# First quad of a two-layer GEGLU kernel: six of its eight weight pieces by casting transfers on the Pool queue, instead of fp32 transfers and casts on chip

## Chip, cores, metric

One core of one Trainium2 chip. The metric is device microseconds (us) of one execution.

## The reference

```python
gate = x @ w_gate                       # x: 8192 tokens x 1024, w_gate, w_up: 1024 x 4096
up = x @ w_up
gate = 0.5 * gate * (1 + np.tanh(np.sqrt(2 / np.pi) * (gate + 0.044715 * gate ** 3)))
h = gate * up
return (h @ w_down).astype(np.float32)  # w_down: 4096 x 1024; all float32
```

## The kernel before

Tokens go through in eight passes of 1024. In the first passes the products are built by a seven-product scheme: it multiplies sums and differences of blocks of x and of the weights. Weight columns are handled in quads of 512 (gate and up each), a quad is two pairs of 256 columns. Only the first quad of the first pass is special, because nothing is on the chip yet: pair 0 is computed by plain products as its pieces arrive, pair 1 already by the scheme, for which VectorE must form sums of x (`sum_x`) and of weights (`sum_w`).

All pieces of that quad are 512 KB of fp32. They come on one hardware queue (issued by SyncE): eight of x, and eight of the weights (gate or up, upper or lower half of K, first or second 256 columns). The weights are staged as fp32 and cast to fp16 by ScalarE or VectorE. Every later quad comes by a transfer that casts on the way, issued by GpSimd (`load_raw`); such a transfer goes through the Pool queue. A one-element GpSimd copy out of a staged piece holds the Pool queue until that piece has landed: a gate.

```python
    def load_first(w, kh, cols):                      # fp32 piece, hardware queue
        nc.sync.dma_start(
            out=staging0(w, kh)[:, :, cols], in_=w_v[w][:, kh * KH : (kh + 1) * KH, cols]
        )

    def cast_first(w, kh, cols, copy=nc.scalar.copy, ks=slice(0, KH)):
        o = raw(0, 0)[:, w, kh * KH : (kh + 1) * KH, cols]
        copy(o[:, ks], staging0(w, kh)[:, ks, cols])
    ...
        # first_pair(): c0, c1 = first, second 256 columns
        ...
        x0_transpose(0, 0, 1, 5, act)
        x0_cast(0, 1, 1)
        x0_transpose(0, 1, 1, 7, dve)
        halves(1)                                     # gate, lower K, c0: cast on ScalarE
        product(1, 0, 1, 0)
        cast_first(1, 1, c0, dve)                     # up, lower K, c0: cast on VectorE
        product(0, 1, 0, 0)                           # first product that needs the lower K
        ...
        for w in range(2):
            cast_first(w, 0, c1)
        nc.gpsimd.tensor_copy(mark, staging0(1, 0)[:, 0, 256:257])   # gate
        load_raw(0, 1)                                # next quad, casting
        ...
        cast_first(0, 1, c1)
        cast_first(1, 1, c1, dve)
        ...
        sum_x(1)
        sum_w(0, 1, 0)
        sum_w(0, 1, 1)
        sum_x(2)
        ...
    # order on the hardware queue
    for kh in range(2):
        for gp in range(2):
            x0_load(0, gp, kh)
        for w in range(2):
            load_first(w, kh, slice(0, 256))
        for gp in range(2):
            x0_load(1, gp, kh)
    for kh in range(2):
        for w in range(2):
            load_first(w, kh, slice(256, 512))
```

## Time and profile before

| | before |
|---|---|
| first three runs | 2253.45, 2254.71, 2254.88 us |
| span of the profiled run | 2252.9 us |
| TensorE busy | 2245.2 us |
| pair 1 starts | 26.80 us |
| last fp32 piece landed (VectorE's wait ends) | 27.61 us |
| the mark M (below) | 38.37 us |
| last piece of the down product of pass 0 starts | 279.21 us |

A line of the timeline holds the start in us, the length in us, engine, source line, operation, output and inputs, and in brackets the idle time before it and what ended it. In these lines `x_b` is x in fp16, `x_sums` its sums and differences, `ring` the buffers of the fp16 weights and of their sums, and `ps` the banks that hold products; `h_a` and `x_sums` also serve as staging for the fp32 pieces. A busy TensorE is not TensorE at its peak, so I compare starts, not busy times. Two starts serve as marks through the whole document. M is the start of the sixteen matmuls with which pair 1 ends and pair 2 begins (eight each); from there to about 279 us the order of work is the same in all kernels. This is M in the timeline of TensorE of the kernel before:

```profile
38.37 3.62 PE L635 MATMUL ps<-x_b,ring 128*128 128x512 f16 x16
```

The second mark is the start at 279 us, the only later point at which TensorE waits in this trace. From it to the last VectorE instruction are 1970.4 us. So M and the start at 279 us tell nearly all that a change in the first quad can do; what is left in the time beside them is the last store and the run itself.

### The profile page before, as it was taken

To read this page: it belongs to the slowest core of one execution; us is meant where nothing else is said; L and a number is where in the kernel's file an instruction comes from. 1 tells how busy PE (TensorE), PEld (TensorE's weight loads), DVE (VectorE), ACT (ScalarE), POOL (GpSimd) and SP (SyncE) were. 2 spreads that over 40 slices of the span, in tenths; PEclk is the share of its full clock that TensorE was granted. 3 is DMA by queue.
4 is the path that set the end of the run, shared out by engine and by line. 5 is a ranking of instruction groups with operands and counts; after the bars stand their busy time and mean duration, and the time that the engine had idled before them with its cause. 6 is when DMAs were issued, how large, how long until landed. Compare 5 with 4: busy or idle time off the path is not lost.

```text
span 2252.9 us, 42769 instructions
## 1 busy us (share of the span) xinstructions
PE 2245.2 (100%) x16616; PEld 1624.1 (72%) x16616; DVE 1560.6 (69%) x2189; ACT 956.4 (42%) x1863; POOL 680.6 (30%) x825
## 2 busy tenths in 40 slices
PE   9999999999999999999999999999999999999999
PEld 4444444444444445888888888888888888888888
DVE  6666458883588755777776677666776667866674
ACT  4443135651355622666125550356404653055520
POOL 1332013330133200555014550255402543044520
PEclk9999999999999999999999999999999999999999
DMA  9898969989999999999998999989999889988876
GB/s 243 164 209 216 288 180 242 262 267 289 247 227 249 279 311 348 328 350 363 302 337 278 316 300 321 321 270 324 307 327 316 286 308 318 318 315 275 283 289 232
DMA packets 309133, 642.46 MB, mean 285 GB/s; under 512 B 79104, under 2 KB 185344, under 8 KB 288384
## 3 DMA queue, kind: packets, MB, share of 16 engines
q1 hardware_dynamic: 254144, 566.57, 73.5%
q0 software_dynamic: 54784, 73.14, 19.3%
q8 instruction: 130, 2.13, 0.4%
q14 instruction: 75, 0.61, 0.1%
HBM read 574.36 MB, written 138.41 MB: 316 GB/s over the span
## 4 chain that ended last, share of the span: by engine, by line
PE 87%; DMA 2%; SPq 1%; DVE 0%; issue 0%; DVEq 0%
PE ps L857 40%; PE ps L1108 20%; PE ps L635 17%; PE ps L1000 10%; DMA wd_quads<-x_sums 1%; SPq L255 0%; DMA ring<-wd_ops 0%; PE ps L1130 0%; DVE x_sums L278 0%; DVE h_a L932 0%; DVE tmp L1140 0%; SPq L496 0%; DVEq L278 0%; SPq L544 0%
## 5 line engine op out<-in xcount | busy, mean ns | idle before, releaser
L857 PEld LDWEIGHTS <-ring 128*128 128x128 f16 x8320 | 814.1, 98 | 94.4
L834 POOL TENSOR_TENSOR h_a<-tmp 128x256 f16<-128x256 f32 x640 | 469.2, 752 | 839.1 <-ACT tmp L822 831.9
L857 PE MATMUL ps<-x_sums,ring 128*128 128x256 f16 x5760 | 655.8, 273 | 0.0
L819 DVE TENSOR_TENSOR tmp<-tmp,ps 128x512 f32<-128x512 f32 x640 | 414.3, 683 | 148.2 <-PE ps L857 100.7
L635 PEld LDWEIGHTS <-ring 128*128 128x128 f16 x2632 | 257.4, 98 | 311.9 <-issue 1.1
L804 ACT COPY tmp<-ps 128x512 f32<-128x512 f32 x520 | 304.5, 586 | 236.7 <-PE ps L857 164.4
L635 PE MATMUL ps<-x_sums,ring 128*128 128x512 f16 x1504 | 340.1, 379 | 0.6 <-DVE x_sums L267 0.4
L822 ACT ACTIVATE tmp<-tmp 128x256 f32<-128x256 f32 x640 | 264.3, 418 | 172.6 <-DVE tmp L817 79.2
L857 PE MATMUL ps<-x_b,ring 128*128 128x256 f16 x2560 | 305.6, 273 | 0.0
L817 DVE TENSOR_TENSOR tmp<-ps,tmp 128x512 f32<-128x512 f32 x240 | 165.4, 689 | 145.2 <-ACT tmp L804 99.9
L635 PE MATMUL ps<-x_b,ring 128*128 128x512 f16 x1128 | 259.3, 379 | 0.1
L661 POOL TENSOR_TENSOR h_a<-tmp 128x512 f16<-128x512 f32 x94 | 145.5, 1548 | 372.9 <-ACT tmp L659 265.6
L1108 PEld LDWEIGHTS <-h_a 128*128 128x128 f16 x2208 | 216.0, 98 | 25.0
L1000 PE MATMUL ps<-ring,h_a 128*128 128x512 f16 x1024 | 222.3, 379 | 0.7 <-DMA ring<-wd_ops 0.7
L1108 PE MATMUL ps<-ring,h_a 128*128 128x256 f16 x1888 | 212.6, 273 | 0.0
L1000 PEld LDWEIGHTS <-h_a 128*128 128x128 f16 x1152 | 112.7, 98 | 136.8 <-DMA ring<-wd_ops 1.2
L654 DVE TENSOR_TENSOR tmp<-ps,tmp 128x512 f32<-128x512 f32 x188 | 127.2, 684 | 113.7 <-ACT tmp L646 112.2
L1238 ACT ACTIVATE tmp<-ps 128x512 f32<-128x512 f32 x60 | 35.3, 598 | 362.5 <-PE ps L1108 274.5
L1171 DVE SCALAR_TENSOR_TENSOR tmp<-ps,tmp 128x512 f32<-128x512 f32 x119 | 80.4, 690 | 95.0 <-PE ps L1108 64.1
L360 DVE TENSOR_TENSOR ring<-ring 128x1024 f16<-128x1024 f16 x188 | 137.6, 745 | 10.5 <-DMA ring<-in_w_up_dram 6.2
L646 ACT COPY tmp<-ps 128x512 f32<-128x512 f32 x188 | 109.8, 586 | 78.5 <-PE ps L635 78.5
L1108 PE MATMUL ps<-ring,x_sums 128*128 128x256 f16 x1120 | 126.3, 273 | 0.0
(105 smaller groups left out, 1538.0 us busy)
## 6 DMA issues: line engine op xcount, KB each, us to landing
ring<-w_ops SPq DMA_DIRECT2D x480, 512.0 KB, 4.8
ring<-wd_quads SPq DMA_DIRECT2D x110, 1024.0 KB, 7.1
ring<-wd_ops SPq DMA_DIRECT2D x35, 1024.0 KB, 7.9
w_ops<-h_s SPq DMA_DIRECT2D x128, 256.0 KB, 6.7
out_dram<-tmp SPq DMA_DIRECT2D x127, 256.0 KB, 6.3
ring<-in_w_gate_dram POOLq DMA_DIRECT2D x23, 1024.0 KB, 10.4
ring<-in_w_up_dram POOLq DMA_DIRECT2D x23, 1024.0 KB, 18.0
wd_quads<-x_sums SPq DMA_DIRECT2D x131, 128.0 KB, 6.6
```

The source lines that it names most:

```text
L360: nc.vector.tensor_tensor(o, a, b, op)
L635: nc.tensor.matmul(ps(b, w), lhs[:, k], rhs[:, k, :], start=(first and k == 0), stop=(k == KH - 1), skip_group_check=True,)
L654: nc.vector.tensor_tensor(o, ps("b", w), o, ADD)
L661: nc.gpsimd.tensor_tensor(hq[TO[n]][:, i, :], tmp[:, t[n, 1]], tmp[:, t[n, 0]], MUL)
L804: nc.scalar.copy(tmp[:, t[o[1]]], ps_all[:, bank[o[2]]])
L817: nc.vector.tensor_tensor(d, b, a, SUB)
L819: nc.vector.tensor_tensor(d, a, b, ADD if o[4] == "add" else SUB)
L822: nc.scalar.activation(d, d, GELU, scale=GSC)
L834: nc.gpsimd.tensor_tensor(h, tmp[:, t[o[1]], MQ : 2 * MQ], g, MUL)
L857: nc.tensor.matmul(ps_all[:, bank[c], w * MQ : (w + 1) * MQ], lhs[:, w, k], rhs[:, k], start=(first and w == 0 and k == 0), stop=(k == KH ...
L1000: nc.tensor.matmul(ps_all[:, bank[b, g]], lhs[:, j, g * P : (g + 1) * P], dc[:, n, :], start=(first and j == 0), stop=(j == NP - 1), skip_ ...
L1108: nc.tensor.matmul(ps_all[:, bank[c], m * MQ : (m + 1) * MQ], lhs[:, j, m * P : (m + 1) * P], rhs[:, j, :], start=(first and j == 0 and m ...
```

## The change

The intent: free ScalarE and VectorE of most casts of the first quad, and let the Pool queue start early instead of after the first quad. Upper K of the first columns stays fp32 on the hardware queue; the other six weight pieces become casting transfers behind two gates, and the next quad's load follows them without a gate.

```diff
+    def load_cast(w, kh, cols):
+        nc.gpsimd.dma_start(
+            out=raw(0, 0)[:, w, kh * KH : (kh + 1) * KH, cols],
+            in_=w_v[w][:, kh * KH : (kh + 1) * KH, cols],
+        )
...
+        nc.gpsimd.tensor_copy(mark, staging0(1, 0)[:, 0, 0:1])
+        for w in range(2):
+            load_cast(w, 1, c0)
+        nc.gpsimd.tensor_copy(mark, x0_f32[1][:, 0, KH * P : KH * P + 1])
+        for kh in range(2):
+            for w in range(2):
+                load_cast(w, kh, c1)
+        load_raw(0, 1)
         warm(7)
...
-        halves(1)
         product(1, 0, 1, 0)
-        cast_first(1, 1, c0, dve)
...
-        for w in range(2):
-            cast_first(w, 0, c1)
-
-        nc.gpsimd.tensor_copy(mark, staging0(1, 0)[:, 0, 256:257])
-        load_raw(0, 1)
...
-        cast_first(0, 1, c1)
-        cast_first(1, 1, c1, dve)
...
-        for w in range(2):
-            load_first(w, kh, slice(0, 256))
+        for w in range(2 if kh == 0 else 0):
+            load_first(w, 0, slice(0, 256))
...
-    for kh in range(2):
-        for w in range(2):
-            load_first(w, kh, slice(256, 512))
```

## The prediction

> **What bounds the kernel now.** I read the page first, then the chain that ended last, then the first 45 us by engine, because everything that the change touches lies there.
>
> ```profile
> PE 2245.2 (100%) x16616; PEld 1624.1 (72%) x16616; DVE 1560.6 (69%) x2189; ACT 956.4 (42%) x1863; POOL 680.6 (30%) x825
> PEclk9999999999999999999999999999999999999999
> ```
>
> TensorE is busy for 2245.2 of 2252.9 us at the full granted clock. All its idle time is 7.7 us, so a change that leaves the matmuls alone can win little. The chain of waits says that it is TensorE all the way from 279 us on, back to back:
>
> ```profile
> 229.17 1.14 DVE h_a L932
> ...
> 270.81 8.35 DMA ring<-wd_ops
> 279.16 0.05 issue
> 279.21 27.80 PE ps L1000 x128
> 307.01 193.39 PE ps L635 x896
> ```
>
> Two readings. First, 193.39 us for 896 matmuls is 0.216 us each; a pair of gate/up columns (56 matmuls) costs 12.1 us when nothing stalls it. Second, one wait (0.7 us, at 279.2 us) hangs on a transfer whose own chain goes back to VectorE work at 229 us. VectorE is busy without a gap there and is itself fed by TensorE's progress, so I take it that a shift made in the first 40 us moves this chain along, rather than being swallowed by it.
>
> The waits of TensorE over the whole run:
>
> ```profile
> PE ps L1284 <- DVE h_s L1287: 1.6, 1, 1.6
> PE ps L314 <- DVE h_a L304: 0.7, 1, 0.7
> PE ps L1000 <- DMA ring<-wd_ops: 0.7, 1, 0.7
> PE ps L1263 <- ACT x_b L317: 0.7, 1, 0.7
> PE ps L635 <- DVE x_sums L267: 0.4, 1, 0.4
> PE ps L635 <- DVE ring L360: 0.2, 1, 0.2
> ```
>
> The last three are in the first quad (the first 512 columns, pairs 0 and 1), and the last two are what the change can reach. "Busy" hides part of them, so I take starts from the timeline of TensorE and VectorE:
>
> ```profile
> 26.80 3.89 PE L635 MATMUL ps<-x_b,ring 128*128 128x512 f16 x16
> 30.53 1.03 PE L635 MATMUL ps<-x_sums,ring 128*128 128x512 f16 x4
> 31.95 2.75 PE L635 MATMUL ps<-x_sums,ring 128*128 128x512 f16 x12 [0.40 <-DVE x_sums L267]
> 34.89 3.64 PE L635 MATMUL ps<-x_sums,ring 128*128 128x512 f16 x16 [0.19 <-DVE ring L360]
> ...
> 27.61 0.69 DVE L340 CAST ring<-h_a 128x1024 f16<-128x1024 f32 x1 [2.99 <-DMA h_a<-in_w_up_dram]
> 28.22 1.22 DVE L267 TENSOR_TENSOR x_sums<-x_b,x_b 128x2048 f16<-128x2048 f16 x1
> 29.35 1.41 DVE L360 TENSOR_TENSOR ring<-ring 128x1024 f16<-128x1024 f16 x2
> ```
>
> From start to start: 16 matmuls took 3.73 us (16 x 0.216 = 3.45, lost 0.28), 4 took 1.42 (0.86, lost 0.56), 12 took 2.94 (2.59, lost 0.35), the next 16 lost 0.03. Pair 1 loses 1.2 us. The cause is seen on VectorE: it idles 2.99 us for the last fp32 piece of the second columns, casts it, and only then starts the chain of sums of which TensorE needs the products.
>
> Before 26.8 us the limit is the transfers. The table by stretches (the columns are busy time of each engine, clock, DMA share, GB/s written):
>
> ```profile
> 3.00:25.00 22.00, 20.60 (x150) 12.84 (x148) 10.72 (x16) 8.47 (x12) 0.10 (x1) 1.00 1.07 366
> 25.00:27.00 2.00, 2.00 (x12) 0.94 (x10) 0.00 (x0) 1.60 (x2) 1.64 (x3) 1.00 0.28 87
> 29.00:37.00 8.00, 7.42 (x34) 3.06 (x33) 7.95 (x11) 2.73 (x6) 0.00 (x0) 1.00 1.24 206
> ```
>
> Sixteen pieces of 512 KB of fp32 come at 366 GB/s, 1.43 us each, without a break until 25. Then the DMA engines are nearly empty for 2 us (87 GB/s), because the casting load of the next quad is only let go at 25.45 us. That load then writes fp16 at 206 GB/s, which is 412 GB/s of fp32 read.
>
> **What the Trainium skill says.** (1) "DMA: Bandwidth & Descriptors", section "SWDGE vs HWDGE vs iDMA": a cast during a transfer exists only on the GpSimd path, and each DMA engine takes turns between the queues of the two paths. The trace agrees in kind: every casting load here is on the Pool queue. How the turns share bytes is what I need and do not have. (2) Same page, "Issuing engines are not separate DMA queues": all queues run on the same 16 engines, so moving pieces to the Pool queue adds no bandwidth. The trace agrees (share above 1 in both stretches). (3) "SBUF — State Buffer", section "SBUF: two separate sides": while VectorE runs a two-port copy or cast, GpSimd cannot write descriptors. No wait of this kind stands in this trace: the issues of the next quad's load took 1.09 and 0.90 us with VectorE idle. After the change the first two issues fall among VectorE's 0.69 us casts.
>
> **The change part by part.**
>
> Removed from ScalarE: the cast of the first gate columns, lower half of K, in two parts (1.14 us at 17.09) and three casts of 1.05 us between 23.3 and 27.3; from VectorE two of 0.69 us (17.52 and 27.61). That is 5.7 us of engine time, but the first ones delay nobody: TensorE's only wait there (0.65 us before 17.25) is for ScalarE's copy of a transpose, which precedes the cast and stays. On the path are the late ones: the copies of the product banks on ScalarE at 28.15 stand behind its last cast (part of the 0.28 lost), and VectorE's sums stand behind its last cast (0.56 + 0.35).
>
> Moved: six of the sixteen pieces go to the Pool queue as casting transfers. Bytes read stay the same. Two (lower K, first columns) are let go when the second weight piece has landed, about 9.0 us; the four of the second columns when the third upper x piece of the lower K has landed, about 18.9 us; the next quad's load follows without a gate.
>
> First columns. From issue to first bytes a Pool transfer took 1.6 us in the quiet case (25.45 to about 27). With some lock time I estimate first bytes at 12 to 13 us. The hardware queue then still owes about three x pieces; from there the two queues share 366 GB/s. What TensorE needs and when: the fourth piece of the first token half by about 15.8 (it has 0.65 us of slack from ScalarE's copy), the gate piece by 18.1, the up piece by 20.3. Data from 12.5 at a 45% share gives the Pool queue 2.55 / 1.43 x 0.45 = 0.8 pieces by 15.05, just what the x piece can bear; at 11 it would take 1.3 and push x back by about 1 us. From 17.25 to 26.8 TensorE is back to back, so a late piece costs one for one. I put the loss at 0.4 us (0 to 1.6).
>
> Second columns. The gate at 18.9 plus four issues and 1.6 us: first bytes near 21, two of the idle DMA microseconds of before moved forward to here. Four pieces take 5.7 us, so the last lands at 27.5 to 28.3 where before it landed at 27.61 and then had to be cast. VectorE does its first x difference in the meantime (1.22 us), so the weight sums start at about 28.0 instead of 29.35. The chain of sums moves forward by 1.1 to 1.3 us, about what pair 1 loses (1.2). I count 1.1 gained.
>
> Next quad's load. It follows in the queue, so the DMA hole at 25 to 27 closes and it lands about 1 us sooner than 39.16. That removes a 1.02 us wait of VectorE that TensorE hardly feels: worth 0.1 at most, not counted.
>
> Sum: 0.4 lost, 1.1 gained: 0.7 us shorter, 2254.7 to 2254.0.
>
> **The rivals.** (a) The Pool queue takes half the bandwidth at once from 11 us. Then the x pieces slip, the products up to 26.8 slip by up to 1.7 us, pair 1 gains 1.2, and the time is 2255.2. For it: both paths are seen active together around 251 us. Against it: of a casting load issued at 230.49, beside a full hardware queue, hardly anything moved until 235. (b) The Pool path is so late that the up piece or the second columns come later than now: each microsecond past 20.3 or past 28.3 is paid in full, 2256 or more. For it is that very case of 230.49; against it, here the hardware queue runs dry by 20. (c) The start gets shorter but the wait at 279 us grows to meet it, because the chain of stores and loads on the Sync queue does not move: then 2254.7. Against it, its root is TensorE-fed. (d) No loss at all in the first columns and the full gain: 2253.4.
>
> **Range and chances.** The three runs of before spread by 1.4 us, as much as the effect. The rivals reach from 2253.4 to 2256; with run noise I take 2252.5 to 2256.0 for 8 in 10. Two per cent is 45 us; the touched stretch is 40 us long, nearly all of it needed work, so a gain of 2% is out of reach and a loss of 2% would need an accident elsewhere. Faster 0.01, same 0.98, slower 0.01.
>
> **What would show it.** Right: in TensorE's timeline the first matmuls of pair 1 start within 1 us of 26.8, no waits on x_sums or ring sums follow in pair 1 (it takes about 12.1 us), the weight sums on VectorE start near 28, the hole of the DMA engines at 25 to 27 is gone, the wait at 279 us is still about 0.7. Wrong: a new wait of TensorE at 16 to 22 us for a cast of x or for a ring piece, of more than 1.2 us; weight sums later than 29.4; first Pool bytes before 11.5 or after 14 us; or a total outside the range with the first 45 us as foretold, which would put the cause after them.

## The result, and the profile after

The changed kernel took 2254.40 us (median of 6, 2253.87 to 2255.00), the kernel before 2254.43 us (median of 6, 2253.45 to 2254.88). The ratio is 1.0001, 95% interval 0.9988 to 1.0014. (A ratio is the mean time of one kernel's fast runs over that of the other's of the same rounds, so not quite the ratio of these medians.) No difference can be seen in the times. The trace shows that this is not "nothing happened": pair 1 starts about 1 us later and takes about 1 us less. The waits of TensorE over the whole run of the changed kernel (total us, times, longest):

```profile
PE ps L1290 <- DVE h_s L1293: 1.6, 1, 1.6
PE ps L314 <- DVE h_a L304: 0.7, 1, 0.7
PE ps L1269 <- ACT x_b L317: 0.7, 1, 0.7
PE ps L1269 <- DMA ring<-in_w_gate_dram: 0.2, 1, 0.2
PE ps L1006 <- DMA ring<-wd_ops: 0.2, 1, 0.2
```

Both waits of pair 1 (for `x_sums` and for `ring` from VectorE) are gone, and one for the gate piece of the weights, straight from a transfer, has come. The timeline of TensorE around it, and through pair 1:

```profile
17.72 1.02 PE L1269 MATMUL ps<-x_b,ring 128*128 128x512 f16 x4 [0.65 <-ACT x_b L317]
18.98 1.90 PE L1269 MATMUL ps<-x_b,ring 128*128 128x512 f16 x8 [0.24 <-DMA ring<-in_w_gate_dram]
...
27.69 3.62 PE L641 MATMUL ps<-x_b,ring 128*128 128x512 f16 x16
31.14 7.07 PE L641 MATMUL ps<-x_sums,ring 128*128 128x512 f16 x32
38.05 3.62 PE L641 MATMUL ps<-x_b,ring 128*128 128x512 f16 x16
```

Pair 1 now runs without a stall: from 27.69 to M are 48 matmuls in 10.36 us, 0.216 each, where before they took 11.57. But pair 1 starts 0.89 later than before. M comes 0.32 earlier. VectorE's weight sums (the 1.42 us line) no longer stand behind a cast, and start 2.8 us sooner than before (29.35 there):

```profile
25.42 1.22 DVE L267 TENSOR_TENSOR x_sums<-x_b,x_b 128x2048 f16<-128x2048 f16 x1
26.58 1.42 DVE L366 TENSOR_TENSOR ring<-ring 128x1024 f16<-128x1024 f16 x2
27.92 1.22 DVE L267 TENSOR_TENSOR x_sums<-x_b,x_sums 128x2048 f16<-128x2048 f16 x1
```

The table by stretches (busy time of each engine, clock, DMA share, GB/s written) shows the hole of before at 25 to 27 us closed: 204 GB/s instead of 87.

```profile
25.00:27.00 2.00, 2.00 (x16) 1.35 (x14) 2.00 (x3) 1.08 (x2) 0.00 (x0) 1.00 1.28 204
```

At 279 us this trace has TensorE start at 278.45 after a shown wait of 0.24 (before: 279.21 after 0.67). From M to there it is 240.40 us, before 240.84. So of the 0.76 us by which the end of all matmuls came forward in these two traces, 0.32 come from the first quad and 0.44 from a shorter wait at 279 us. The latter varies from run to run, as before_again shows below.

### The profile page after: what moved, and what is told of

Read it like the earlier page. It is cut to its first block, busy times and chain, and to the rows that moved or that the text cites. A ratio compares the mean times of both kernels' runs of the same rounds, so it can differ in the third digit from the quotient of the medians.

```text
span 2252.5 us, 42767 instructions
## 1 busy us (share of the span) xinstructions
PE 2245.4 (100%) x16616; PEld 1621.4 (72%) x16616; DVE 1561.7 (69%) x2187; ACT 950.9 (42%) x1858; POOL 680.3 (30%) x832
## 4 chain that ended last, share of the span: by engine, by line
PE 87%; DMA 2%; SPq 1%; DVE 0%; issue 0%; DVEq 0%
PE ps L863 40%; PE ps L1114 20%; PE ps L641 17%; PE ps L1006 10%; DMA wd_quads<-x_sums 1%; SPq L255 1%; DMA ring<-wd_ops 0%; PE ps L1136 0%; DVE x_sums L278 0%; DVE h_a L938 0%; DVE tmp L1146 0%; SPq L502 0%; DVEq L278 0%; SPq L550 0%
```

## The experiments

Each kernel ran 5 times in rounds with the kernel before, on one chip per group, and once under the profile. All gave correct results. This table sums them up. "Weight sums start" is the start of VectorE's first sums of weights for pair 1 (the line of 1.4 us); "time" is the mean of a kernel's runs minus the mean of the kernel before of the same rounds (9 runs in each of the three groups), with its standard error worked out from the spread of both.

| kernel | pair 1 starts | weight sums start | M | start at 279 | M to there | idle shown there | time |
|---|---|---|---|---|---|---|---|
| before | 26.80 | 29.35 | 38.37 | 279.21 | 240.84 | 0.67 |  |
| before_again | 27.57 | 29.44 | 38.45 | 278.67 | 240.22 | 0 | -0.26 ± 0.26 |
| after | 27.69 | 26.58 | 38.05 | 278.45 | 240.40 | 0.24 | +0.18 ± 0.29 (6 and 6 runs) |
| after_again | 27.51 | 27.08 | 37.87 | 277.87 | 240.00 | 0 | -0.53 ± 0.29 |
| second_only | 26.99 | 29.96 | 38.98 | 278.98 | 240.00 | 0 | -0.24 ± 0.45 |
| first_only | 29.67 | 29.14 | 40.03 | 280.25 | 240.22 | 0 | +2.29 ± 0.38 |
| shift_nine | 29.60 | 28.48 | 39.96 | 279.97 | 240.01 | 0 | +1.40 ± 0.24 |
| early_gate | 26.84 | 28.65 | 37.67 | 277.68 | 240.01 | 0 | -1.03 ± 0.39 |
| fill | 27.56 | 27.34 | 37.92 | 278.56 | 240.64 | 0.48 | -0.71 ± 0.28 |
| second_early | 27.53 | 26.74 | 37.89 | 278.90 | 241.01 | 0.85 | -0.58 ± 0.38 |
| one_gate | 26.74 | 26.40 | 37.10 | 277.11 | 240.01 | 0 | -0.60 ± 0.22 |
| one_gate_order | 27.00 | 26.30 | 37.36 | 277.37 | 240.01 | 0 | -0.84 ± 0.16 |
| before_order | 27.21 | 28.29 | 37.58 | 278.70 | 241.12 | 0.94 | +0.14 ± 0.49 |

Two things can be read off the table. First, M is in all 13 traces, within 0.02 us, the later of two points: pair 1's start plus 10.36 (its 48 matmuls without a stall), or the start of the weight sums plus 9.02. The second point sets M in before, before_again, second_only and early_gate, the first in the other nine. So a change helps only if it moves the later of the two. Second, from M to the start at 279 us it is 240.0 us in six traces. In the other seven it is 0.2 to 1.1 us more, and that is the real wait there; the idle that the profile shows is about 0.2 less (the ends of matmuls in it are modelled).

Theory after the first look: the change takes pair 1's stalls away and pays for it with a late gate piece. Rivals: the late start of pair 1 is another effect of the change (TensorE's first products were slower in its trace); a gain at the start is swallowed at 279 us; the gain is not due to the casts but to VectorE's order.

### after_again: the changed kernel once more

No edit.

> The changed kernel once more, for the spread. Theory (gain 1.2 in pair 1, loss 0.4 from a late gate piece, and a late switch of TensorE to its full rate that is chance): pair 1 starts at 27.2 or 27.7 depending on the switch (first four products slow or not), pair 1 takes 12.1, the wait for the gate piece near 18.7 is there again (0.2 shown, 0.4 lost); time 2253.5 to 2254.5. Rival (the slow first products are caused by the change): the first 12 products take 3.3 us again and pair 1 starts at 27.7 again.

The first twelve products took 3.22 us, as in the first trace of the changed kernel (3.33) and not as in that of before (2.81). But shift_nine and early_gate, the same until there but for early_gate's earlier gate, took 2.81 and 2.78. So the slow start is not the change; it comes and goes. The Trainium skill says as much ("TensorE: Matmul & The Clock Gate", "Part 1: The HAM clock gate (the "warmup" mystery)"): the moment at which TensorE goes to its full rate hangs on a free-running window and varies by ±500 ns. Here the spread is wider: the twelve products take 2.75 to 3.33 us, and second_early and before_order are at the full rate long before them (their eight transposes at 5.6 and 5.5 us take 0.62 us, in the other traces 1.03 to 1.04). It does not add to the loss either: in shift_nine TensorE was early, and waited longer for the same gate piece; its next products start at 18.95, here at 18.80, in the first trace at 18.98. **In the changed kernel the landing of the gate piece, near 18.9, sets pair 1's start, and with it M.** (In shift_nine, before its extra matmuls, pair 0 ends 0.86 later than in before.) M is 37.87 here, 0.5 to 0.6 before the two traces of before.

### second_only: only the second columns by casting transfers

```diff
-        nc.gpsimd.tensor_copy(mark, staging0(1, 0)[:, 0, 0:1])
-        for w in range(2):
-            load_cast(w, 1, c0)
...
+        halves(1)
         product(1, 0, 1, 0)
+        cast_first(1, 1, c0, dve)
...
-        for w in range(2 if kh == 0 else 0):
-            load_first(w, 0, slice(0, 256))
+        for w in range(2):
+            load_first(w, kh, slice(0, 256))
```

> Only the second columns (and the next quad's load behind them) come by casting transfers; all of the first columns as before. Theory: no wait of TensorE on a ring piece at 18 to 19, pair 1 starts at 26.8 (27.3 if the switch to the full rate is late), pair 1 takes 12.1 to 12.3, so pair 2 starts at about 38.9 to 39.4 against 40.1 before; time 1.2 below before, 2253.2. Rival (a gain at the start is swallowed later): pair 2 starts earlier but the time is that of before within 0.3.

Pair 1 started where it should (26.99), but its stalls were there, and larger: M at 38.98 is 0.6 later than before. The table by stretches of this run shows the reason in its last two columns, the share of the DMA engines and GB/s:

```profile
18.00:19.00 1.00, 1.00 (x7) 0.44 (x5) 0.35 (x2) 0.42 (x1) 0.00 (x0) 1.00 1.04 381
19.00:20.00 1.00, 1.00 (x6) 0.44 (x5) 0.61 (x1) 0.00 (x0) 0.97 (x2) 1.00 0.61 213
20.00:21.00 1.00, 1.00 (x12) 0.74 (x11) 0.75 (x1) 0.33 (x1) 1.00 (x2) 1.00 0.00 0
21.00:22.00 1.00, 1.00 (x7) 0.41 (x6) 0.03 (x1) 1.00 (x2) 1.00 (x2) 1.00 0.40 32
```

The hardware queue ran dry at 19.5, the gate opened at 19.03, the first casting transfer was issued at 19.60, and its first bytes came at 21.3. The DMA engines lost nearly 2 us, and VectorE's weight sums started at 29.96. My theory that the second columns alone bring 1.2 is wrong: with this gate they bring a loss. Whether they gain if the Pool queue has bytes to move when the hardware queue ends, second_early tests.

### first_only: only the lower K of the first columns by casting transfers

```diff
-        nc.gpsimd.tensor_copy(mark, x0_f32[1][:, 0, KH * P : KH * P + 1])
-        for kh in range(2):
-            for w in range(2):
-                load_cast(w, kh, c1)
-        load_raw(0, 1)
...
+        for w in range(2):
+            cast_first(w, 0, c1)
+        nc.gpsimd.tensor_copy(mark, staging0(1, 0)[:, 0, 256:257])
+        load_raw(0, 1)
...
+        cast_first(0, 1, c1)
+        cast_first(1, 1, c1, dve)
...
+    for kh in range(2):
+        for w in range(2):
+            load_first(w, kh, slice(256, 512))
```

> Only the lower half of K of the first columns comes by casting transfers; the second columns as fp32 and cast on chip, as before. Theory: the wait for the gate piece stays (0.4), pair 1 keeps its stalls (13.0 to 13.5 us), pair 2 starts at about 40.5 against 40.1; time 0.4 above before, 2254.7 to 2254.9. Rival (the first columns gain by the freed engines): pair 1 starts at 26.8 or earlier.

Much worse than expected: the time is 2.3 us above before. TensorE's waits:

```profile
PE ps L1269 <- DMA ring<-in_w_up_dram: 1.7, 1, 1.7
...
PE ps L1269 <- DMA ring<-in_w_gate_dram: 0.8, 1, 0.8
```

The gate piece comes as late as in the changed kernel (the products that need it start at 19.07). The up piece is late by 1.7 more, because here the hardware queue never runs dry: four fp32 pieces of the second columns, needed later, go on sharing with it. With the gates of the changed kernel, neither part of the change is of use by itself. Moving the second columns away is what lets the first columns' up piece through, and the first columns on the Pool queue are what keeps it running for the second. The stalls of pair 1 did vanish here, only because it starts at 29.67, after the weight sums have begun (29.14).

### shift_nine: TensorE delayed on purpose

```diff
             product(1, kh, 1, 1)
+        warm(9)          # 9 matmuls into a bank that is overwritten next
         ps_free.clear()
```

> The changed kernel with 9 matmuls more (into a bank that is overwritten next) between the first pair and pair 1: TensorE is 1.94 us later from there. Theory that a shift passes through to the end: time 1.9 above the changed kernel, about 2256.3. Rival (transfers set the point at 279 us and swallow shifts): pair 2 starts 1.9 later, the wait at 279 us shrinks to nothing, and the time rises by less than 1.5.

M is 1.9 to 2.1 later than in the two traces of the changed kernel, the start at 279 us 1.5 to 2.1 later, and the mean time 1.93 above that of after_again in the same rounds, for 1.94 us put in. A shift in the first 40 us passes through to the end, and an earlier M passes to 279 us as well (M to there is 240.0 us in shift_nine and in one_gate, whose M lie 2.9 us apart). The rival that the wait at 279 us swallows it is out for this size.

### before_again: the kernel before once more

No edit.

> The kernel before once more, for the spread of its profile. Theory: pair 1 starts at 26.8 to 27.3 (depending on when TensorE reaches its full rate, seen in the first 12 products), pair 1 loses 1.2 again, pair 2 starts at 40.0 to 40.6; whether TensorE waits at 279 us is chance, so the end can move by up to 0.8; ratio 1.000. Rival (the wait at 279 belongs to the kernel before): 0.7 again.

The wait at 279 us is nearly absent (M to there is 240.22 us, so 0.2 instead of 0.8), so its size is not a property of the kernel before. Over 13 traces it comes in seven (0.2 to 1.1 us by the table) and shows no tie to how early TensorE arrives: one_gate arrives first of all, at 277.11, and does not wait. I could not find what decides it; with M fixed it moves the end by up to 1.1 us, as much as the effect under study. And pair 1 starts 0.77 later than in the first trace, since another transfer was the late one:

```profile
22.01 0.69 DVE L304 TENSOR_SCALAR h_a<-h_a 128x1024 f16<-128x1024 f32 x1 [2.25 <-DMA h_a<-in_x_dram]
...
27.70 0.69 DVE L340 CAST ring<-h_a 128x1024 f16<-128x1024 f32 x1 [2.31 <-DMA h_a<-in_w_up_dram]
```

The last x piece was taken up at 22.01 instead of 20.34, the last weight piece at 27.70 (27.61 before), and M is the same within 0.08. **So in both traces of the kernel before, M is set by the landing of the last fp32 piece and by what VectorE does behind it (cast, x difference, sums)**, not by pair 1's start. This corrects my sum: the 1.2 of pair 1 and the loss in pair 0 are no two independent terms. The change takes M from one limit (the weight sums behind the last fp32 piece, 38.4) to another (pair 1's start behind the gate piece, 37.9 to 38.05).

### early_gate: the first gate opens one piece sooner

```diff
-        nc.gpsimd.tensor_copy(mark, staging0(1, 0)[:, 0, 0:1])
+        nc.gpsimd.tensor_copy(mark, staging0(0, 0)[:, 0, 0:1])
```

> The changed kernel, its two first casting transfers let go one weight piece sooner (near 7.9 instead of 9.3 us). If the 4 us from issue to first bytes is a latency: first Pool bytes near 12.3, the gate piece 1.5 earlier, no wait on it at 18.1, but the x pieces slip; pair 1 starts at 26.9 to 27.3 and the time falls by 0.4 to 0.8 against the changed kernel. Rival (first Pool bytes come when the hardware queue reaches a certain transfer): again at 14.0, nothing changes.

The issues of the first casting transfer in the timelines of GpSimd, first of the changed kernel, then of this one:

```profile
10.00 0.94 POOL L339 DMA_DIRECT2D ring<-in_w_gate_dram  x1
...
8.32 0.94 POOL L339 DMA_DIRECT2D ring<-in_w_gate_dram  x1 [0.37 <-issue]
```

By the DMA view in narrow windows, the first bytes moved at 14.4 in the changed kernel and at 12.7 here. So it is a delay of 4.4 us from the issue, which moves with the issue, and not an event in the hardware queue. With that queue empty or nearly so it is 1.7 to 1.8 us (second_only: 19.60 to 21.3; the next quad's load of the kernel before: 25.45 to 27.2). It is no constant beside a busy queue either: in second_early, where the hardware queue runs dry by 20 us, it is 2.3 us (17.01 to 19.3). The wait for the gate piece is gone, pair 1 starts at 26.84, and the time is 1.0 below before. What now sets M is the weight sums (28.65, behind the late second gate): pair 1 loses 0.5. How the two queues share is seen in the transfers of this run from 13 to 18 us (packets, MB written, share of 16 engines):

```profile
DMA packets 1257, 1.54 MB, mean 307 GB/s; under 512 B 48, under 2 KB 660, under 8 KB 1257
...
q1 hardware_dynamic: 629, 1.22, 72.3%
q0 software_dynamic: 628, 0.31, 45.3%
```

629 packets to 628: one for one. But the packets are not of one size. A packet of x on the hardware queue is 1.22 MB / 629 = 1.9 KB, one of the Pool queue writes 0.5 KB, having read 1 KB. So the Pool queue gets 0.62 of 1.84 MB read, a third, and a piece of 512 KB needs 4 us there instead of 1.43. First bytes at 14.4 and 4 us give about 18.4 for the changed kernel, as an estimate; the profile has the gate piece landed at 18.9 (8.9 us after its issue), so some 0.5 us are not accounted for. In first_only, where the hardware queue later carries weight pieces in 1 KB rows, I find 509 to 508 packets between 18 and 21 us and equal bytes read.

### fill: transposes in front of the products that wait

```diff
         product(1, 0, 1, 0)
+        x0_cast(1, 0, 1)
+        x0_transpose(1, 0, 1, 7, act)
         product(0, 1, 0, 0)
         product(0, 1, 0, 1)
-        x0_cast(1, 0, 1)
-        x0_transpose(1, 0, 1, 7, act)
         x0_cast(1, 1, 1)
```

> The changed kernel with TensorE's transposes of the third-landing x piece (and VectorE's cast of it) moved in front of the two products that wait for the gate piece. Theory (TensorE stands idle for the gate piece): the same landing near 18.9, the transposes fit into the wait, pair 1 starts 0.45 earlier, at 27.1 to 27.2; time 0.4 below the changed kernel, 2253.5 to 2253.8. Rival: the piece of x is not there in time and TensorE waits for it instead, nothing won.

Not conclusive by itself: TensorE reached its full rate late (3.27 us for the first twelve products), and came to this place 0.29 later than in the first trace of the changed kernel.

```profile
18.01 1.02 PE L1269 MATMUL ps<-x_b,ring 128*128 128x512 f16 x4 [0.65 <-ACT x_b L317]
18.87 0.61 PE L314 MATMUL ps<-identity,h_a 128*128 128x128 f16 x8
19.31 3.62 PE L1269 MATMUL ps<-x_b,ring 128*128 128x512 f16 x16
```

No wait for the gate piece is left, and pair 1 started 0.13 earlier there, so against its own arrival it won 0.42, close to the 0.45 expected. The time (0.7 below before) agrees, with an idle of 0.48 at 279 us against it.

### second_early: the second columns alone, with an earlier gate

```diff
-        nc.gpsimd.tensor_copy(mark, x0_f32[1][:, 0, KH * P : KH * P + 1])
+        nc.gpsimd.tensor_copy(mark, staging0(0, 1)[:, 0, 0:1])
```

(against second_only)

> Only the second columns by casting transfers, let go when the gate piece of the lower K has landed (about 16.0 instead of 18.9 us), so that the Pool queue has bytes to move when the hardware queue runs dry near 19.5. Theory (the hole of the DMA engines at 19.5 to 21.8 cost the gain in second_only): first bytes at 19 to 20, the weight sums start near 27.7 instead of 29.96, pair 1 takes 12.1 to 12.4 and starts at 26.8 to 27.0, pair 2 starts at 39.0 to 39.3; time 1.1 below before. Rival (casting transfers of 512 byte rows are slow themselves): sums later than 29 in spite of it.

The hole is gone, the weight sums start at 26.74, and pair 1 has no stall. M is 37.89, where 37.3 to 37.6 was expected (pair 2's start of 39.0 to 39.3, less 8 x 0.216), because pair 1 started late: the last x piece landed at 21.69, as in before_again, with casting transfers already in the queue beside it.

```profile
PE ps L314 <- DVE h_a L304: 2.0, 4, 0.9
...
PE ps L1006 <- DMA ring<-wd_ops: 0.8, 1, 0.8
```

So in this trace the second columns alone are worth 0.5 at M, as much as the whole change, if their gate is right. The time, 0.6 below before, has the longest but one idle at 279 us in it.

### one_gate: no second gate

```diff
-        nc.gpsimd.tensor_copy(mark, x0_f32[1][:, 0, KH * P : KH * P + 1])
```

(against early_gate)

> early_gate with the second gate dropped: all six casting pieces and the next quad's load stand one behind the other in the Pool queue from 8 us on. Theory (the Pool queue is first in, first out, so the second columns do not compete before the first are through, and early_gate lost 0.5 in pair 1 because the late second gate left a dip at 20 us): pair 1 starts at 26.8 to 27.1 as there, the weight sums start at 27.5 to 28.0 instead of 28.65, pair 1 takes 12.1, pair 2 starts 0.4 earlier than in early_gate, near 38.9; time 2253.1 to 2253.4, about 1.3 below before. Rival (a longer Pool queue takes more from the hardware queue): an x piece is late and pair 1 starts after 27.5.

M is 37.10 (and the start at 279 us 277.11), the earliest of all, 1.3 before that of the kernel before, where 38.9 less 8 x 0.216, so 37.2, was expected. The weight sums start at 26.40 (28.65 in early_gate). So the second gate was not needed: the pieces behind took nothing away from those ahead or from x (VectorE takes up the last x piece at 19.45, 19.43 in early_gate), as they must if the Pool queue is first in, first out. The time is 0.6 below before. This trace is one of the two with waits in the second pass (0.25 and 0.18 at 412 us, for VectorE): from its start at 277.11 to the end it takes 1971.2 us, 0.8 of the gain lost again, as far as this one trace goes.

### one_gate_order: and TensorE's order mended

```diff
         x0_cast(1, 1, 0)
+        x0_cast(0, 0, 1)
         x0_transpose(1, 1, 0, 7, dve)
-        for c in (lo, hi):
-            for j in range(2):
-                product(1, 0, 0, j, c)
-        x0_cast(0, 0, 1)
+        for j in range(2):
+            product(1, 0, 0, j, lo)
         x0_transpose(0, 0, 1, 5, act)
+        for j in range(2):
+            product(1, 0, 0, j, hi)
         x0_cast(0, 1, 1)
```

(against one_gate)

> one_gate, and TensorE gets half of a product between the two groups of transposes before 17 us, so that ScalarE's copy (the 0.65 wait at 17.25) is covered. If data are there: that wait shrinks to 0.2 or less and pair 1 starts at 26.2 to 26.5; but then the weight sums bind and pair 1 takes 12.4 to 12.6, so pair 2 starts at 38.7 to 38.9; time 0.1 to 0.3 below one_gate. Rival (the gate piece or x lands too late): a wait for a transfer takes the place of the copy and nothing is won.

The rival held. The wait of 0.65 for ScalarE's copy is gone, and a wait for the gate piece has taken its place; pair 1 starts no sooner:

```profile
PE ps L1269 <- DMA ring<-in_w_gate_dram: 0.6, 1, 0.6
```

It is nevertheless the kernel with the clearest time: all five runs (2253.12 to 2253.38) lie below all nine of before (2253.62 to 2254.93), 0.84 on average. It is faster than the kernel before by 0.04%. The changed kernel's 11 runs (2253.65 to 2255.00) also lie above its five, but they were taken in other rounds. I do not claim that it beats one_gate or early_gate.

### before_order: no casting transfer, only VectorE's order

```diff
-        cast_first(0, 1, c1)
-        cast_first(1, 1, c1, dve)
-        ps_free.clear()
-        ps_free.extend(range(8))
         sum_x(1)
+        cast_first(0, 1, c1)
+        cast_first(1, 1, c1, dve)
+        ps_free.clear()
+        ps_free.extend(range(8))
```

(against the kernel before)

> The kernel before, no casting transfer added; only VectorE's first x difference is moved in front of its cast of the last second-column piece, for which it idles 2 to 3 us. Theory that most of the gain in pair 1 is the order of VectorE and not the casts: the weight sums start at 28.3 instead of 29.4, pair 2 starts at 39.1 to 39.4 instead of 40.1, time 0.8 to 1.0 below before. Rival (the landing of the fp32 pieces and the casts on ScalarE and VectorE bind): pair 2 starts within 0.3 of before.

VectorE now does its first x difference in the time in which it waited for the last fp32 piece:

```profile
24.95 1.22 DVE L267 TENSOR_TENSOR x_sums<-x_b,x_b 128x2048 f16<-128x2048 f16 x1
...
27.49 0.69 DVE L340 CAST ring<-h_a 128x1024 f16<-128x1024 f32 x1 [1.33 <-DMA h_a<-in_w_up_dram]
28.29 1.42 DVE L360 TENSOR_TENSOR ring<-ring 128x1024 f16<-128x1024 f16 x2
```

The piece lands as late as ever (27.49), the cast is still there, but the sums behind it start at 28.29, and M is 37.58: 0.8 before that of the kernel before, and ahead of the changed kernel's. Pair 1's start (27.21) sets it here, no longer the sums. **In these single traces one moved line does more for M than the whole change.** In the time nothing of it can be seen (+0.14 ± 0.49): the profiled run was its slowest (2255.79), with the longest wait at 279 us (0.94 shown) and two waits of 0.3 in the second pass (at 445 and 478 us), and 1972.1 us from the start at 279 us to the end. The other four runs are between 2253.38 and 2254.86. Whether this kernel loses its gain more often than the others do is open.

## Why the prediction was right, and where it was not

The time lay in the stated range (2254.4 in 2252.5 to 2256.0) and in the class of 98%. That says little: a range of 3.5 us around an expected gain of 0.7 holds "no change" as well, and the gain itself cannot be seen in the times. In the profiled runs more of the shorter span came from the wait at 279 us (0.44) than from the first quad (0.32), and that was luck. Of the prediction's own signs of being wrong one came true (first Pool bytes after 14 us), and of its signs of being right two failed (weight sums near 28, a wait at 279 us of about 0.7). By its steps:

- **What bounds the kernel, and that a shift passes to the end**: right. shift_nine got 1.93 for 1.94 put in.
- **Pair 1 gains 1.1**: it lost its 1.2 us of stalls (48 matmuls in 10.36 us). The wait named, TensorE for VectorE's sums behind the last fp32 piece, is right: where the sums come earlier, the stalls go. But the cast was not the costly part: before_order keeps the casts and takes only the x difference out of the chain behind the piece, and the stalls go as well. The sum for the landing was wrong (first bytes at 21 and 5.7 us make 26.7, not 27.5 to 28.3). The time of the second gate was wrong, too: I took the x piece's landing from the trace of before (18.9), but two weight pieces ahead of it had left the hardware queue, and the gate opened at 16.67. So the sums started at 26.58 or 27.08, not at 28.0 (in shift_nine, with the same loads, at 28.48); all this was early enough that M did not hang on it.
- **First columns lose 0.4 (0 to 1.6)**: the loss was 0.7 to 0.9 against the first trace of before (from 0.1 earlier to 0.1 later against before_again, which waited for a late x piece of its own). Three terms failed. First bytes came at 14.2 to 14.4, not at 12 to 13: the 1.7 to 1.8 us of the quiet case became 4.4 us beside a full hardware queue. I had seen such a delay in the trace (the issue at 230.49, first bytes at 234.5) and put it among the rivals. The share was a third of the bytes read, not 45%. And the piece that was late was the gate piece, not x: no x piece held TensorE up after the first transposes. Had I worked with 14.4 and a third, I would have had the gate piece's bytes in at about 18.4, and the wait.
- **The sum, 0.7 less**: M came 0.3 to 0.6 earlier (two traces on each side). The times give -0.17 ± 0.17 (mean of 11 runs of the changed kernel, minus that of all 38 of before); they do not contradict the traces and cannot confirm them. The two terms should not have been added, since M is the later of two limits: the loss counts only from where pair 1's start becomes the later one.
- **Rivals**: (a) a half share from 11 us did not happen. (b) was nearest, by its mechanism: a late Pool path, here at the gate piece, which I had not put first. (c) is out for the shift, but the wait at 279 us that I took for fixed at 0.7 varies from run to run and has the size of the effect. (d) no loss in the first columns: this is what early_gate and one_gate reached, and the full gain with it at M in one_gate.

What stays open: what decides the wait at 279 us and the rarer waits of the second pass, why the last x piece comes 1.3 to 1.7 us late in some runs, and what the casting transfer waits for in its 4.4 us.

## What to carry to other kernels

Before moving work to another queue, ask what its first bytes wait for and how it shares with a queue that is full: here a small-row queue got a third of the bytes and started 4.4 us after the issue, so its gates had to open earlier than a quiet trace suggests. Look first whether the waiting engine has other work that could go in front of the wait: at M, a moved line brought as much as a rebuilt load path (one trace; the times show neither). And where two limits lie within 1 us of each other, don't add the effects of a change: find which limit sets the mark that follows.

## What the Trainium skill lacked or had wrong

- "DMA: Bandwidth & Descriptors", "Latency and other measured facts" has the first byte of a transfer issued by GpSimd at about 1 us. These runs show 1.7 to 1.8 us from the start of the issue with the hardware queue empty or nearly so, and 4.4 us beside a full one (10.00 to 14.4, 8.32 to 12.7). The page does not have the second case.
- Same page, "Queues, rings and completion order": an engine takes turns at packets of some 9 to 17 descriptors. In the profile's count the turns are one packet for one (629 to 628, 509 to 508), with one row per packet, so that the queue with the smaller rows gets fewer bytes: a third of those read, beside rows of 2 KB. The page does not say this consequence. (Whether the profile counts packets as the page does, no run shows.)
- "SBUF — State Buffer", "SBUF: two separate sides": the page has GpSimd shut out while VectorE runs a two-port copy, and its example is a transfer that grows from about 0.62 to 3.1 us. Here the cost was smaller: a gate's one-element copy took 0.63 instead of 0.19 us beside a cast of 0.69, and an issue beside a cast up to 1.05 us (changed kernel, at 18.69), where the like took 0.74. It does not explain the 4.4 us: in early_gate the gate's copy took 0.19, and the delay was the same.
- "TensorE: Matmul & The Clock Gate", Part 1: the ±500 ns of the switch to the full rate is too small for these 13 traces. Two are at the full rate from 5.5 us on; in the others the last matmul at the slow rate starts between 8.3 and 10.0 us.
